# Feed-forward with tokens stationary: gate and up columns side by side as one 512-column moving operand, the result transposed, and conversions ahead moved behind the activation

## The chip, the cores and the metric

The kernel runs on one core of one Trainium2 chip. The metric is the device time of one execution in microseconds (us). Three runs of the kernel before took 1474.69 to 1477.07 us, with a median of 1476.81.

## What is computed

The reference is a stack of three blocks on 256 tokens of width 1024, all in float32. The first two are "macaron" layers: a feed-forward, a mixer, a feed-forward, each between RMS norms, with a residual sum. The mixer of layer 0 joins stick-breaking attention and a causal convolution; that of layer 1 is gated linear attention. The third block has adaptive modulation from a condition vector, one mixer of sparse attention and retention, and one feed-forward. So there are five feed-forwards, and all have the same form:

```python
def swiglu(x, w_in, w_out):
    a, b = jnp.split(x @ w_in, 2, axis=-1)
    return (jax.nn.silu(a) * b) @ w_out
```

Here `x` is 256 x 1024, the hidden width is 2816 (11 x 256), `a` is called the gate and `b` the up projection. In the third block gate and up are two weights. Every weight is used once, so all weights pass from HBM through the core once.

## The kernel before

**Precision.** A float32 product is made of three TensorE products: each operand is split in `hi` (a copy rounded to the engine's faster 32-bit type) and `lo` (what is left). `mm3` (L268) makes hi x hi, hi x lo and lo x hi into one sum. Weights are split as they arrive: `feed_cv` (L230) lets ScalarE write `hi` (L246) and VectorE `lo` (L247). Activations are kept transposed, features on partitions, as `xh` and `xl`.

**The weight stream.** `weight_plan` (L101) lists all weights as chunks of at most 128 x 1024 elements in the order of their use. `feed_dma` (L221) issues a chunk's load on SP's queue into one of four raw buffers (`NRAW`). `feed_cv(n)` converts all chunks up to `n`, and a chunk's load is issued when the buffer four chunks back is split. `nxt` (L251) hands out the next chunks. With `ahead` on, it also lets conversions run on, by one more than it hands out, up to a lead of `pos["depth"]`, 14 chunks in a feed-forward (28 buffers `s4` for hi and lo). `catch_up(n)` (L265) queues up to `n` more conversions within the same lead. The order of the calls is the order of the work on each engine: the schedule is manual, and an engine does its instructions in the order in which the program wrote them.

**A feed-forward** (`ffn`, L666) goes through the 2816 hidden columns in 11 blocks `j` of 256. For block 0, tokens are stationary: 128 tokens by 128 features of `xh` or `xl` are the weights of the array, and 256 columns of the gate or up chunk move (L684 to L688). The result has tokens on partitions; its product `u` is transposed on TensorE (L721) and split into `hh` and `hl` (`split_sb`, L531). For blocks 1 to 10, the weight chunk is stationary, 128 features by 128 hidden columns, and 256 tokens move (`wproj2`, L536): 48 matmuls for the gate (`pa`) and 48 for up (`pb_`). The result has hidden columns on partitions, as the output projection needs it, so nothing is transposed. The norm's factor per token, `x.r`, is then needed along the columns: `nz.rows()` (L426) spreads it with four matmuls into `x.rb`, VectorE multiplies the gate by it (L729), ScalarE applies SiLU (L730), VectorE multiplies by up (L745). The last feed-forward has a norm that is already applied (`x.r` and `x.rb` are `None`), and skips the factor.

The output projection of block `j - 1` stands in block `j`, behind its matmuls (`fpart`, L706): 24 matmuls with `hh` or `hl` stationary and 512 output columns moving, into four PSUM banks `f`. The projections of the last three blocks (`NH`) come at the end as `pieces`, first those of token half 0, then those of half 1. `boundary` (L491) takes these pieces and puts the next stage's norm, transposes and first conversions among them. In `each`, three steps of a side job (the modulation vector, `ada_step`, L619) are queued at the start of a block.

**PSUM** has eight banks `pb` of 128 x 512. The small tiles of a feed-forward (`sg`, `u`, `hh`, `hl`, the side job's) share 16 buffers `s2`.

## Time and profile before

| | |
|---|---|
| Median of three runs | 1476.81 us |
| The profiled execution | 1476.34 us |
| Its span, first to last instruction | 1474.6 us |
| TensorE busy | 1440.0 us, 98% |
| VectorE busy | 1000.3 us, 68% |
| ScalarE busy | 764.5 us, 52% |
| GpSimd busy | 259.5 us, 18% |
| HBM read | 277.90 MB, 189 GB/s over the span |
| mean granted TensorE clock | 0.992 |

In the profile PE is TensorE, PEld its weight loads, ACT ScalarE, DVE VectorE, POOL GpSimd, and SP the engine whose queue issues the weight loads. L12 is line 12 of the program. Matmuls are pipelined, and a matmul's record is longer than the time until the next one can start; the pace is therefore read from one start to the next, or as the length of a stretch over the number of matmuls in it. The trace's times are counted from the first instruction.

### The profile page before, as it was taken

What the parts mean: (1) busy time and instruction counts of PE and PEld (TensorE: products, weight loads), DVE (VectorE), ACT (ScalarE), POOL (GpSimd) and SP (SyncE); (2) the same over time, 40 slices, a digit from 0 to 9 for tenths busy, and PEclk for the clock granted to TensorE, in tenths of its full rate; (3) what the DMA queues carried; (4) which work ended last, traced back from release to release, by engine and by line L of the source; (5) the groups of instructions that cost most, each with busy time, mean ns of one, the idle gap of its engine ahead of it and who ended that gap; (6) DMA issues with size and microseconds to landing.
All of it is one profiled execution on the core that took longest, in us unless ns stands there. A gap on an engine that the chain in (4) does not pass through costs nothing. (4 is left out here: it accounts for less than half of the span.)

```text
span 1474.6 us, 24444 instructions
## 1 busy us (share of the span) xinstructions
PE 1440.0 (98%) x9623; PEld 1314.8 (89%) x9623; DVE 1000.3 (68%) x1348; ACT 764.5 (52%) x1182; POOL 259.5 (18%) x339
## 2 busy tenths in 40 slices
PE   9999998699999999999999999999999999999997
PEld 8999988579999999999888899998988877899997
DVE  6777658977776667766577677765596865566542
ACT  6554356756543364443663655545643664565431
POOL 3010025812000031000234110001132230200001
PEclk9999999899999999999999999999999999999999
DMA  8887644227887568775542488763565554387540
GB/s 276 275 279 250 188 144 130 71 86 241 286 260 234 172 223 265 231 237 173 163 144 72 129 282 261 259 207 116 164 198 169 165 170 157 101 262 240 183 129 29
DMA packets 194948, 281.03 MB, mean 191 GB/s; under 512 B 12381, under 2 KB 148241, under 8 KB 194834
## 3 DMA queue, kind: packets, MB, share of 16 engines
q1 hardware_dynamic: 184386, 248.87, 53.5%
q0 software_dynamic: 10048, 30.03, 6.2%
q8 instruction: 75, 1.23, 0.3%
q10 hardware_dynamic: 400, 0.57, 0.1%
q14 instruction: 39, 0.32, 0.1%
HBM read 277.90 MB, written 1.05 MB: 189 GB/s over the span
## 5 line engine op out<-in xcount | busy, mean ns | idle before, releaser
L247 DVE TENSOR_TENSOR lo<-raw,hi 128x1024 fp32r<-128x1024 f32 (+1 forms) x461 | 549.5, 1219 | 237.2 <-ACT hi L246 204.0
L246 ACT ACTIVATE hi<-raw 128x1024 fp32r<-128x1024 f32 (+1 forms) x472 | 477.4, 1037 | 206.4 <-PE pb L271 69.2
L269 PE MATMUL pb<-xh,hi 128*128 128x256 f32 x1968 | 558.4, 284 | 0.1
L271 PE MATMUL pb<-xh,lo 128*128 128x256 f32 x1968 | 556.8, 283 | 0.0
L270 PE MATMUL pb<-xl,hi 128*128 128x256 f32 x1968 | 556.8, 283 | 0.0
L269 PEld LDWEIGHTS pb<-xh,hi 128*128 128x128 f32 x1968 | 376.3, 191 | 3.4 <-issue 1.3
L270 PEld LDWEIGHTS pb<-xl,hi 128*128 128x128 f32 x1968 | 376.4, 191 | 2.0
L271 PEld LDWEIGHTS pb<-xh,lo 128*128 128x128 f32 x1968 | 376.3, 191 | 0.2
L269 PE MATMUL pb<-hi,hh 128*128 128x512 f32 x440 | 172.1, 391 | 0.0
L270 PE MATMUL pb<-lo,hh 128*128 128x512 f32 x440 | 171.7, 390 | 0.0
L271 PE MATMUL pb<-hi,hl 128*128 128x512 f32 x440 | 171.2, 389 | 0.0
L626 POOL DMA_DIRECT2D ada<-in_w_ada_dram x96 | 51.8, 542 | 452.0 <-PE pb L271 278.8
L532 ACT ACTIVATE hh<-u 128x512 fp32r<-128x512 f32 x50 | 31.6, 632 | 134.4 <-DVE u L745 132.5
L271 PEld LDWEIGHTS pb<-hi,hl 128*128 128x128 f32 x440 | 82.6, 188 | 17.5
L269 PEld LDWEIGHTS pb<-hi,hh 128*128 128x128 f32 x440 | 82.8, 188 | 15.9
L270 PEld LDWEIGHTS pb<-lo,hh 128*128 128x128 f32 x440 | 82.8, 188 | 15.3
L269 PE MATMUL pb<-hi,xh 128*128 128x512 f32 x224 | 91.5, 408 | 0.0
L271 PE MATMUL pb<-hi,xl 128*128 128x512 f32 x224 | 88.1, 393 | 0.0
L270 PE MATMUL pb<-lo,xh 128*128 128x512 f32 x224 | 88.0, 393 | 0.0
L730 ACT ACTIVATE sg<-sg 128x512 f32<-128x512 f32 x40 | 25.3, 632 | 109.8 <-DVE sg L729 109.8
L631 DVE SCALAR_TENSOR_TENSOR adacc<-ada,sc,adacc 128x512 f32<-128x512 f32 x84 | 63.0, 750 | 2.0
L331 POOL TENSOR_TENSOR rs_y<-rs_v,mhalf 128x1 f32<-128x1 f32 x30 | 16.9, 564 | 259.0 <-DVE rs_v L330 258.0
(314 smaller groups left out, 1726.2 us busy)
## 6 DMA issues: line engine op xcount, KB each, us to landing
raw<-in_ffn_w_in_dram SPq DMA_DIRECT2D x176, 512.0 KB, 5.0
raw<-in_ffn_w_out_dram SPq DMA_DIRECT2D x88, 512.0 KB, 4.7
raw<-in_w_in_dram SPq DMA_DIRECT2D x56, 512.0 KB, 4.2
ada<-in_w_ada_dram POOLq DMA_DIRECT2D x96, 256.0 KB, 4.5
raw<-in_gla_w_in_dram SPq DMA_DIRECT2D x24, 512.0 KB, 4.2
raw<-in_w_ffn_gate_dram SPq DMA_DIRECT2D x22, 512.0 KB, 4.8
raw<-in_w_ffn_up_dram SPq DMA_DIRECT2D x22, 512.0 KB, 5.0
raw<-in_w_ffn_down_dram SPq DMA_DIRECT2D x22, 512.0 KB, 4.0
```

Of the source, the lines that this page charges most:

```text
L246: act.activation(hv, r, AF.Copy)
L247: lo_on.tensor_tensor(lv, r, hv, op=ALU.subtract)
L269: pe.matmul(o, lh, rh, start=start, stop=False)
L270: pe.matmul(o, lh, rl, start=False, stop=False)
L271: pe.matmul(o, ll, rh, start=False, stop=stop)
L331: pool.tensor_tensor(y, v, mhalf[:, :1], op=ALU.pow)
L532: act.activation(hi, full, AF.Copy)
L626: pool.dma_start(t, w_ada[kt * 128:(kt + 1) * 128, cb * 512:(cb + 1) * 512])
L631: dve.scalar_tensor_tensor(ada["acc"], in0=t, scalar=sc[:, kt:kt + 1], in1=ada["acc"], op0=ALU.mult, op1=ALU.add)
L730: act.activation(sg, sg, AF.Silu)
```

## The change

Four things change together.

- The plan of a feed-forward: in place of chunks `fa` (gate) and `fb` (up) of 4 x 128 features by 256 columns, there are four chunks `fi` a block, each 2 x 128 features by 512 columns, 256 gate columns beside the 256 up columns of the same block. Each is loaded by two DMAs of 256 KB.
- All blocks are computed as block 0 was, with tokens stationary, and gate and up move together: one matmul has 512 columns and fills one bank. Per block and token half the bank holds gate | up.
- `gated(j, p)` applies SiLU with the norm's factor per partition and makes the product; `turn(j)` transposes it into one bank and splits it. `turn(j - 1)` stands behind the first chunk of block `j` (`TJ = 0`). For block 10 it is done in two halves among the pieces. `nz.rows()` is no longer called here.
- Conversions ahead: the calls of the first and the last chunk of a block (`ahead=i not in (TJ, 3)`) queue none beyond their own chunk; instead `catch_up(2)` stands behind `turn` and behind `gated`.

In the prologue of the kernel, block 0's first chunks are converted in slices of 512 columns accordingly.

```diff
 PRF = (0, 0, 2)
 CT, CS = (2, 2), (0, 1)
 CU = (0, 1, 2)
+TJ = 0
 DEPTH = (14, (10, 9), (10, 10), (10, 10))
 NT = 2
 LO, CL = ((1, 0), (1, 1)), 1
@@ -120,13 +121,11 @@
 
     def ffn(wa, wb, b0, wo):
         for j in range(NJ + 1):
-            if j == 0:
-                for k0 in (0, 4):
-                    cols("fa", wa, 0, 256, k0, 4)
-                    cols("fb", wb, b0, 256, k0, 4)
-            elif j < NJ:
-                tall("fa", wa, j * 256)
-                tall("fb", wb, b0 + j * 256)
+            for k0 in range(0, 8 if j < NJ else 0, 2):
+                rs = slice(k0 * 128, (k0 + 2) * 128)
+                src = [w[rs, c0:c0 + 256].rearrange("(k p) c -> p k c", p=128) for w, c0 in ((wa, j * 256),
+                                                                                             (wb, b0 + j * 256))]
+                plan.append(("fi", src, 2, 512))
             for i in range(2 if 0 < j <= NJ - NH else 2 * NH if j == NJ else 0):
                 cols("fo", wo, 0, 1024, 2 * (min(j - 1, NJ - NH)) + i, 1)
 
@@ -223,7 +222,12 @@
             i = pos["dma"]
             _, src, nk, n_ = plan[i]
             r = raws.tile([128, WCH], F32, tag="raw", name="raw")
-            nc.sync.dma_start(r[:, :nk * n_].rearrange("p (k c) -> p k c", k=nk), src)
+            rv = r[:, :nk * n_].rearrange("p (k c) -> p k c", k=nk)
+            if isinstance(src, list):
+                for g in range(2):
+                    nc.sync.dma_start(rv[:, :, g * 256:(g + 1) * 256], src[g])
+            else:
+                nc.sync.dma_start(rv, src)
             raw_t[i] = r
             pos["dma"] += 1
 
@@ -667,41 +671,53 @@
         x = nz.x
         hp = {}
 
-        def split_h(u):
-            hh, hl = s2([128, 2, S], F32R, name="hh"), s2([128, 2, S], F32R, name="hl")
-            split_sb(hh, hl, u)
-            return hh, hl
-
-        chs = nxt("fa", "fb", "fa", "fb", ahead=False)
-        pt, u0 = [], []
+        chs = nxt("fi", "fi", "fi", "fi", ahead=False)
+        p0 = []
         for t in range(2):
-            p = pp()
+            p = pb()
             ks = KO if t and not nz.early else range(8)
             for n_, kk in enumerate([*ks, None]):
-                for g in range(2):
-                    if kk is not None:
-                        hi, lo = chs[2 * (kk // 4) + g]
-                        pe.matmul(p[g][:, :S], x.h[:, kk, tsl(t)], hi[:, kk % 4], start=n_ == 0, stop=False)
-                        pe.matmul(p[g][:, :S], x.h[:, kk, tsl(t)], lo[:, kk % 4], start=False, stop=False)
-                    if n_:
-                        k0 = ks[n_ - 1]
-                        pe.matmul(p[g][:, :S], x.l[:, k0, tsl(t)], chs[2 * (k0 // 4) + g][0][:, k0 % 4], start=False,
-                                  stop=kk is None)
+                if kk is not None:
+                    hi, lo = chs[kk // 2]
+                    pe.matmul(p, x.h[:, kk, tsl(t)], hi[:, kk % 2], start=n_ == 0, stop=False)
+                    pe.matmul(p, x.h[:, kk, tsl(t)], lo[:, kk % 2], start=False, stop=False)
+                if n_:
+                    k0 = ks[n_ - 1]
+                    pe.matmul(p, x.l[:, k0, tsl(t)], chs[k0 // 2][0][:, k0 % 2], start=False, stop=kk is None)
                 if t == 0 and n_ in TB:
                     nz.trans(1, [TB.index(n_)])
-            pt.append(p)
+            p0.append(p)
             if t == 0:
                 nz.spread(1)
                 nz.evac(1)
                 nz.scale(1)
                 catch_up(CU[2])
-        for t in range(2):
-            sg = s2([128, S], name="sg")
-            act.activation(sg, pt[t][0][:, :S], AF.Silu, scale=1.0 if x.r is None else x.r[t])
-            u = s2([128, S], name="u")
-            dve.tensor_tensor(u, sg, pt[t][1][:, :S], op=ALU.mult)
-            u0.append(u)
         f = None
+        us = {}
+
+        def gated(j, p):
+
+            sg, u = s2([128, 2, S], name="sg"), s2([128, 2, S], name="u")
+            for t in range(2):
+                act.activation(sg[:, t], p[t][:, :S], AF.Silu, scale=1.0 if x.r is None else x.r[t])
+                dve.tensor_tensor(u[:, t], sg[:, t], p[t][:, S:], op=ALU.mult)
+            us[j] = u
+
+        def turn(j, ts=(0, 1)):
+
+            u = us[j]
+            if 0 in ts:
+                hp[j] = s2([128, 2, S], F32R, name="hh"), s2([128, 2, S], F32R, name="hl")
+            hh, hl = hp[j]
+            pr = pb()
+            pv = two(pr)
+            for t in ts:
+                for i in range(2):
+                    pe.transpose(pv[:, i, tsl(t)], u[:, t, i * 128:(i + 1) * 128], ident)
+            sl = slice(ts[0] * 128, (ts[-1] + 1) * 128)
+            split_sb(hh[:, :, sl], hl[:, :, sl], pv[:, :, sl])
+            if 1 in ts:
+                us.pop(j)
 
         def fpart(j, i, ch, t, n):
             hh, hl = hp[j]
@@ -709,29 +725,23 @@
             mm3(f[t][n], hh[:, i, tsl(t)], hl[:, i, tsl(t)], ch[0][:, 0, cs], ch[1][:, 0, cs],
                 j == 0 and i == 0, j == NJ - 1 and i == 1)
 
+        gated(0, p0)
+        p0 = None
         for j in range(1, NJ):
             if each and j > 1:
                 each()
-            pa = wp("fa", x)
-            if j == 1:
-                nz.rows()
-                pr = pb()
-                for i in range(2):
-                    for t in range(2):
-                        pe.transpose(pr[:, i * S + t * 128:i * S + (t + 1) * 128], u0[t][:, i * 128:(i + 1) * 128],
-                                     ident)
-                hp[0] = split_h(two(pr))
-            chb = nxt("fb", "fb")
-            sg = s2([128, 2, S], name="sg")
-            if x.rb is None:
-                act.activation(sg, two(pa), AF.Silu)
-            else:
-                dve.tensor_tensor(sg, two(pa), bc2(x.rb), op=ALU.mult)
-                act.activation(sg, sg, AF.Silu)
-            pb_ = pb()
-            wproj2(pb_, chb, x)
+            pj = pp()
+            for i in range(4):
+                ch = nxt("fi", ahead=i not in (TJ, 3))
+                for t in range(2):
+                    smm(pj[t], t, ch, 2 * i, 8, x.h, x.l)
+                if i == TJ:
+                    turn(j - 1)
+                    catch_up(2)
             if f is None:
                 f = [pp(), pp()]
+            gated(j, pj)
+            catch_up(2)
             if j < NJ - NH + 1:
                 for i in range(2):
                     ch = nxt("fo")
@@ -741,16 +751,17 @@
                 hp.pop(j - 1)
             if each:
                 ada_sum()
-            u = s2([128, 2, S], name="u")
-            dve.tensor_tensor(u, sg, two(pb_), op=ALU.mult)
-            hp[j] = split_h(u)
         cho = nxt(*["fo"] * (2 * NH))
 
         def pieces(t):
             def part(j, n):
                 for i in range(2):
                     fpart(j, i, cho[2 * (j - NJ + NH) + i], t, n)
-            return [(lambda j=j, n=n: part(j, n)) for n in range(2) for j in range(NJ - NH, NJ)]
+            todo = [(lambda j=j, n=n: part(j, n)) for n in range(2) for j in range(NJ - NH, NJ)]
+            if t == 0:
+                todo[1:1] = [lambda: turn(NJ - 1, (0,))]
+                todo[3:3] = [lambda: turn(NJ - 1, (1,))]
+            return todo
         return f, pieces
 
 
@@ -1526,14 +1537,15 @@
     nz.trans(0)
     feed_dma(4)
     for i in range(4):
-        cv_t[i] = tuple(s4([128, WCH], F32R, name=n_).rearrange("p (k c) -> p k c", k=4) for n_ in ("hi", "lo"))
+        cv_t[i] = tuple(s4([128, WCH], F32R, name=n_).rearrange("p (k c) -> p k c", k=2) for n_ in ("hi", "lo"))
     for k in range(8):
         nz.evac1(0, k)
-        for i in (k // 4 * 2, k // 4 * 2 + 1):
-            hi, lo = (z[:, k % 4] for z in cv_t[i])
-            rv = raw_t[i][:, k % 4 * 256:(k % 4 + 1) * 256]
-            act.activation(hi, rv, AF.Copy)
-            (pool if i % 2 and k in KS else dve).tensor_tensor(lo, rv, hi, op=ALU.subtract)
+        hi, lo = (z[:, k % 2] for z in cv_t[k // 2])
+        rv = raw_t[k // 2][:, k % 2 * 512:(k % 2 + 1) * 512]
+        act.activation(hi, rv, AF.Copy)
+        for g in range(2):
+            c = slice(g * 256, (g + 1) * 256)
+            (pool if g and k in KS else dve).tensor_tensor(lo[:, c], rv[:, c], hi[:, c], op=ALU.subtract)
     for i in range(4):
         raw_t.pop(i)
     pos["cv"] = 4
```

## Rows read from the trace of the kernel before

**Rows 1.** The page: busy us (share) of TensorE; granted clock in 40 slices.
```profile
PE 1440.0 (98%) x9623; PEld 1314.8 (89%) x9623; DVE 1000.3 (68%) x1348; ACT 764.5 (52%) x1182; POOL 259.5 (18%) x339
...
PEclk9999999899999999999999999999999999999999
```

**Rows 2.** Stretches of TensorE: start:end, length, busy (instructions touched), clock, DMA, GB/s.
```profile
395.41:406.92 11.51, 11.51 (x97) 1.00 0.88 284
...
200.38:204.47 4.09, 4.09 (x20) 1.00 0.71 231
...
805.97:811.55 5.58, 5.58 (x27) 1.00 0.07 23
```

**Rows 3.** Stretches from block 1, four feed-forwards: PE, PEld, DVE, ACT, POOL, clock, DMA.
```profile
22.80:58.80 36.00, 36.00 (x260) 34.03 (x259) 24.96 (x26) 21.40 (x25) 6.11 (x12) 1.00 0.88 289
343.50:379.50 36.00, 36.00 (x259) 34.08 (x258) 26.01 (x28) 20.35 (x24) 3.22 (x6) 1.00 0.91 301
848.34:884.34 36.00, 36.00 (x260) 34.08 (x259) 26.50 (x30) 19.23 (x22) 3.62 (x7) 1.00 0.89 286
1291.17:1327.17 36.00, 36.00 (x260) 34.08 (x259) 24.63 (x24) 22.14 (x26) 0.00 (x0) 1.00 0.84 269
```

**Rows 4.** Timeline of TensorE at transposes: start, us, operation, tiles, count.
```profile
538.82 0.78 PE L432 MATMUL pb<-dg,ones 128*128 128x128 f32 x4
539.43 0.60 PE L721 MATMUL pb<-ident,u 128*128 128x128 f32 x4
...
805.62 0.60 PE L525 MATMUL pb<-ident,oy 128*128 128x128 f32 x4
805.97 0.48 PE L269 MATMUL pb<-hi,xh 128*128 128x512 f32 x1
...
1296.93 0.60 PE L721 MATMUL pb<-ident,u 128*128 128x128 f32 x4
1297.28 0.36 PE L269 MATMUL pb<-xh,hi 128*128 128x256 f32 x1
```

**Rows 5.** Lines L700 and L702: count, duration in ns (min/median/max), first and last start.
```profile
L700 ACT ACTIVATE sg<-pb,rs_y x8: 457/469/477, 22.0 to 848.5; 128x256 f32<-128x256 f32 x8
...
L702 DVE TENSOR_TENSOR u<-sg,pb x10: 410/414/421, 23.5 to 1292.2; 128x256 f32<-128x256 f32 x10
```

**Rows 6.** Timeline of ScalarE: start, us, operation, count, idle before and its releaser.
```profile
7.99 0.42 ACT L1535 ACTIVATE hi<-raw 128x256 fp32r<-128x256 f32 x1 [1.08 <-DMA raw<-in_ffn_w_in_dram]
...
373.94 1.06 ACT L246 ACTIVATE hi<-raw 128x1024 fp32r<-128x1024 f32 x1 [2.80 <-DMA raw<-in_ffn_w_out_dram]
...
378.39 0.63 ACT L730 ACTIVATE sg<-sg 128x512 f32<-128x512 f32 x1 [1.89 <-DVE sg L729]
...
504.87 1.99 ACT L246 ACTIVATE hi<-raw 128x1024 fp32r<-128x1024 f32 x2
```

**Rows 7.** Timeline of VectorE: splits of weights, merged runs of up to four.
```profile
49.78 1.23 DVE L247 TENSOR_TENSOR lo<-raw,hi 128x1024 fp32r<-128x1024 f32 x1 [0.24 <-ACT hi L246]
...
371.17 1.22 DVE L247 TENSOR_TENSOR lo<-raw,hi 128x1024 fp32r<-128x1024 f32 x1 [0.26 <-ACT hi L246]
...
505.95 2.36 DVE L247 TENSOR_TENSOR lo<-raw,hi 128x1024 fp32r<-128x1024 f32 x2 [0.26 <-ACT hi L246]
...
873.47 4.62 DVE L247 TENSOR_TENSOR lo<-raw,hi 128x1024 fp32r<-128x1024 f32 x4
...
1313.51 4.63 DVE L247 TENSOR_TENSOR lo<-raw,hi 128x1024 fp32r<-128x1024 f32 x4 [0.26 <-ACT hi L246]
```

**Rows 8.** The raw buffers, 344 to 380 us: issue ns (min/median/max); landing.
```profile
L226 SPq DMA_DIRECT2D raw<-in_ffn_w_in_dram x12: 367/373/379, 344.3 to 376.3; - x12
...
DMA to landing us min/median/max: 3.5/5.3/6.8
```

**Rows 9.** Timeline of TensorE in the mixer of layer 0.
```profile
291.68 0.79 PE L271 MATMUL pb<-hi,ml 128*128 128x512 f32 x1 [2.52 <-DVE ml L898]
```

**Rows 10.** The stretch behind that wait, columns as in rows 3.
```profile
292.27:295.68 3.41, 3.41 (x9) 2.63 (x8) 3.41 (x6) 3.36 (x6) 3.10 (x5) 0.50 0.00 0
```

## Prediction

> **What bounds the kernel now.** I read the page's busy times first: TensorE is busy for 1440.0 of 1474.6 us, and the granted clock stands at 9 in nearly every slice [rows 1]. So a change counts where it alters the time of TensorE's own stream, or stops that stream. Next I read that stream by stretches [rows 2]. A feed-forward's block of 256 hidden columns is 96 matmuls of 256 columns in 11.51 us: 120 ns from one to the next. Matmuls of 512 columns with tokens stationary, which another stage runs already, take 4.09 us for 18: 227 ns each. No pause is left inside such a block, so the change cannot remove one; it can only make the stream shorter and put pauses into it. Last I read the other engines where a feed-forward begins: there, DMA is busy 84 to 91% of the time [rows 3], so weights come about as fast as they can be loaded, and ScalarE waits for them (2.80 us in one place [rows 6]).
>
> **What the stream loses and gains.** Each of the five feed-forwards has 11 blocks. A block's 96 matmuls become 48 (8 contraction steps, 2 token halves, 3 products) of 512 columns: 48 x 0.227 = 10.90 us for 11.51, so 0.61 us less, and 55 x 0.61 = 33.6 us less in all [rows 2].
>
> The result now has tokens on partitions, so it must be transposed. Before, only block 0 did this, in 5 groups of four transposes. Now there are 50 such groups, and 10 of two for the last blocks. Four transposes take 0.35 us until the next matmul starts, between wide matmuls as between narrow ones [rows 4]. Behind them the wide matmuls need a moment to regain their pace: 24 of them take 5.58 us and not 24 x 0.227 = 5.45 [rows 2], so a group costs 0.48 us. With narrow neighbours I estimate 0.43 (some 0.08 us late behind it), and 0.61 is what four other matmuls of 128 columns took, the row scale's, with a wait in them [rows 4]; these are my two ends. A group of two saves two steps of 0.11 us: 0.27 us. Sum: 50 x 0.48 + 10 x 0.27 - 5 x 0.43 = 24.5 us more (22 to 32).
>
> The call that spreads the row scale along columns goes in the four feed-forwards that have it: 0.61 us each [rows 4], 0.43 where nothing waits; I take 4 x 0.5 = 2.0 us less. TensorE's stream is thus 33.6 + 2.0 - 24.5 = **11.1 us shorter** (4 to 14).
>
> A word on the Trainium skill: its page "TensorE: Matmul & The Clock Gate", section "Back-to-back issue gap", gives an isolated matmul's gap as N / 2.4 plus 2.5 ns, by which doubling the width would save 2.5 ns for each pair, 2640 x 2.5 ns = 6.6 us in place of 33.6, and the change would lose some 16 us by its transposes. The rows disagree: 2 x 120 - 227 leaves 13 ns for a pair, with both widths read at the full clock.
>
> **ScalarE, VectorE and the queues.** ScalarE's SiLU becomes two of 128x256 for one of 128x512: 0.47 us each [rows 5] for 0.63 [rows 6], 0.3 us more in a block. VectorE loses the multiplication by the row scale and makes the product in two pieces of 0.41 us [rows 5]. Neither engine is the bound over a block; only the moment counts at which each reaches this work. Both work in program order, and between these operations stand the weight conversions (hi on ScalarE, 1.06 us [rows 6]; lo on VectorE, 1.23 us [rows 7]), each of which can wait for its DMA, or for a buffer that TensorE frees.
>
> The price is set by a new wait. In the kernel before, block j's product was needed, split, when its output projection began: one block later. Now TensorE itself transposes it after the first chunk of the next block, that is 24 x 0.227 + 12 x 0.227 = 8.2 us after the block's end (2.7 us after block 0 and after block 9, behind which no output projection stands). Queued behind a late transpose is all of TensorE's stream.
>
> I number a feed-forward's chunks from 0; block 0 takes 0 to 3, a later block four and then two for an output projection. By the calls, chunks up to 6 are converted ahead when block 1 begins (up to 5 in the first feed-forward). In block 1 six more are queued ahead of its SiLU (two by catch_up, two by each of the two calls with ahead on), and six behind it; in block 2 six ahead again. So block 2's SiLU stands behind chunk 24 (23 in the first). Until the lead reaches the limit of 14 chunks, these wait for DMA, not for buffers.
>
> When does chunk 24 land? Four raw buffers go round, so its load starts when chunk 20 has been split: at 372.39 us in the second feed-forward, 878.09 in the fourth and 1318.14 in the fifth, and 51.01 for chunk 19 in the first (start and duration of [rows 7]). From issue to landing it takes 5.3 us (3.5 to 6.8) [rows 8]. From there hi takes 1.06, lo 1.25 behind it, and the two products 0.8 (the SiLUs, 0.94, run beside lo): 3.1 us. Ready at 59.4, 380.8, 886.5 and 1326.5. Block 2's transposes are due 36.4 us after block 1 begins (2 x 10.9 + 2 x 5.45 + 2.7 + 2 x 0.48), and block 1 begins 0.6 us earlier than before, at the start of each window of [rows 3] less 0.6: due at 58.6, 379.3, 884.1 and 1327.0. TensorE would wait 0.8, 1.5, 2.4 and 0 us. But the first conversions of block 1 now stand behind block 0's transposes, some 2.8 us later than before; followed from chunk to chunk, in steps of 5.3 us of load and 2.3 of conversion, about 1.0 us of that is left at chunk 20. I take 1.8 + 2.5 + 3.4 + 0.5 = **8.2 us of waiting** (0.6, if loads come at 3.5 us and nothing is late; 21, at 6.8 us and the whole 2.8 late). The third feed-forward follows another one and begins with four more chunks converted, so nothing is late there. From block 3 on the limit of 14 chunks lets only as much be queued as TensorE has freed, and the wait is over.
>
> The second new wait is at the end. After block 10 its second SiLU runs, then catch_up queues two conversions, and only then comes the split of the transposed half. From the end of block 10: SiLU until 0.8 us, two hi until 2.7 (1.99 for two [rows 6]) and two lo, from 1.8 on, until 4.2 (2.36 for two [rows 7]); then half of hl, 0.4: 4.6 us. TensorE is there after two pieces of 6 x 0.227 and two transpose groups, at 3.3 us, and asks for hl with its third matmul, at 3.8. That is 0.8 us, in four feed-forwards (the last has no weights left to convert): **3.2 us** (0 to 6). Before, the split stood ahead of these two conversions, so that cover goes.
>
> Two DMAs for one chunk: an issue holds SP's queue for 0.37 us [rows 8], and beside the loads SP issues only a few constants; the packets keep their 1 KB rows. The second half starts 0.4 us later, which is inside the bounds above. In the prologue, block 0's first conversions need one buffer instead of two (ScalarE waited 1.08 us for the second [rows 6]), but a piece is twice as wide: I take 0, from -1 to +1 us. PSUM: a block's two banks and one for transposes fit into the four that the outputs leave, each freed before it is asked for, so 0; if not, it is the price of the transposes' own wait.
>
> **Sum.** -11.1 + 8.2 + 3.2 = +0.3 us. The profiled execution took 1476.34 us (span 1474.6), 0.5 us under the median of 1476.81. 1476.3 + 0.3 = 1476.6: **about 1477 us, no change that can be told**; 0.2% (2.95 us) is about what a measurement of this kernel can tell from none, so "same" runs from 1473.9 to 1479.8. The forecast's own range is 1471 to 1484.
>
> **Rivals.**
> *The product is always in time.* Loads come faster than 5.3 us, as the row-scale steps no longer stop the conversions. For it: before, ScalarE sat idle for 1.89 us at 378.39 until the scaled SiLU could run [rows 6], a stop that goes. Against it: DMA is 84 to 91% busy. Then -11.1 and the ends' 0 to 3.2: **1467 us** (1465 to 1469).
> *The product is late and the clock falls* (the other side). One mechanism: block 2's SiLU behind chunk 24. It decides from a total wait of 11.3 us there on (1479.8 - 1476.3 + 11.1 - 3.2). With 6.3 us from issue to landing, between the median and the worst, and 1.5 us of lateness, the waits are 3.3 + 4.0 + 4.9 + 2.0 = 14.2 us. In another stage TensorE waited 2.52 us [rows 9], and behind that its granted clock was 0.50 (the 1.2 GHz level), nine matmuls in 3.41 us [rows 10] for 2.0; at two places that is 2.8 us. -11.1 + 14.2 + 3.2 + 2.8 = 9.1: **1485 us**.
> *The width saves less here.* At the 5.58 us for 24 of [rows 2], which stand behind transposes, a block takes 11.16 us, and 55 blocks save 19 us in place of 33.6: **1491 us**. Against it: the pace settles within a few matmuls.
> *The change does not do what it says.* Half as many matmuls and four transposes a block follow from the loops, so that is excluded; that the conversions stand behind the activation's work holds for the two calls named, not for the six conversions ahead of it, which the forecast prices.
>
> **Chances.** Forecast 0.51 (0.06 of it faster than 1473.9, 0.32 same, 0.13 slower); in time 0.26, all faster; late with the clock 0.21 and less saved 0.02, all slower. Faster 0.06 + 0.26 = 0.32; same 0.32; slower 0.13 + 0.21 + 0.02 = 0.36. The range takes in most of both sides: 1465 to 1489.
>
> **What would show it.** 48 matmuls of 512 columns in about 10.9 us a block; four transposes in 0.35 us; no row-scale matmuls in the feed-forwards; a TensorE wait of 1 to 4 us ahead of block 2's transposes, released by VectorE's u, in the first, second and fourth feed-forward and none in the third; about 0.8 us before the last block's first piece, released by hl. I am wrong if the blocks take 11.2 us or more, if those waits are missing, or if one stands in every block.

## The result, and the profile after

The changed kernel takes 1487.9 us (median of 4 runs, 1484.2 to 1490.3) for 1476.8 before: a ratio of 1.0073, 95% interval 1.0054 to 1.0091. It is slower by 11.1 us, where the forecast said no change that can be told (1477 us, its own range 1471 to 1484; the wide range, 1465 to 1489, holds it). The time lies where the rival put it that has the product late and the clock low behind it (1485 us); two things that also stopped TensorE, a PSUM bank ahead of block 3 and the late split of block 1, were not in that rival. The profiled execution took 1487.56 us, span 1485.8.

The page of the changed kernel: TensorE's busy time, and its granted clock in 40 slices.
```profile
PE 1432.4 (96%) x7167; PEld 1192.4 (80%) x7167; DVE 978.5 (66%) x1359; ACT 765.2 (51%) x1221; POOL 258.4 (17%) x339
...
PEclk9999999999999999999999999999999999999999
```
Against [rows 1]: TensorE has 7.6 us less to do in a span that is 11.2 us longer. So the stream did become shorter, and some 19 us of standing still came in. The row of the clock hides what follows, since a slice is 37 us long.

Where it stands still shows when each feed-forward is one stretch, from its first transposes of the residual to those ahead of the next stage. Columns: start:end, length, TensorE's busy time, clock, DMA share, GB/s. The kernel before:
```profile
5.32:196.76 191.44, 190.08 (x1335) 0.99 0.77 249
327.49:516.97 189.48, 189.48 (x1345) 1.00 0.72 232
516.97:706.62 189.65, 189.65 (x1346) 1.00 0.70 221
832.34:1022.04 189.70, 189.70 (x1348) 1.00 0.69 219
1271.58:1466.99 195.41, 194.53 (x1373) 1.00 0.51 159
```
The changed kernel, the same five:
```profile
5.26:205.65 200.39, 189.79 (x843) 0.98 0.75 237
336.39:529.76 193.37, 189.15 (x853) 0.99 0.71 227
529.76:717.32 187.56, 186.97 (x854) 1.00 0.71 224
841.37:1034.65 193.28, 189.55 (x855) 0.99 0.67 214
1284.65:1477.94 193.29, 192.41 (x885) 1.00 0.51 161
```
The third and the fifth are 2.1 us shorter each. The first, second and fourth, which follow the start or a mixer, are 9.0, 3.9 and 3.6 us longer: length less busy time is 10.6, 4.2 and 3.7 us there, and was 1.4, 0 and 0. The mixers between them are not touched; the one of layer 1 is 1.7 us shorter here, and was as short in a run of the kernel before (e4).

A block that nothing disturbs, as stretches of TensorE in the third feed-forward (columns as in [rows 3]): 12 matmuls, then 36 behind the four transposes, then the whole block with its output projection.
```profile
561.98:564.70 2.72, 2.72 (x13) 2.20 (x12) 2.15 (x3) 1.39 (x2) 0.00 (x0) 1.00 0.90 299
565.05:573.35 8.30, 8.30 (x40) 6.85 (x38) 7.48 (x9) 5.20 (x6) 1.07 (x2) 1.00 0.93 289
561.98:578.79 16.81, 16.81 (x78) 13.90 (x76) 13.43 (x15) 10.14 (x12) 1.61 (x3) 1.00 0.94 306
```
2.72 + 0.35 + 8.30 = 11.37 us for 48 wide matmuls and four transposes, where 96 narrow ones took 11.51 [rows 2]. These terms of the sum hold, and so does the group's 0.35 of [rows 4].

TensorE's own rows where a feed-forward stumbles, in the changed kernel (start, us, operation, tiles, count, idle before and its releaser): the first (50 to 70 us), the second (381 and 392) and the fourth (887 to 898), and the end of the first (194 to 195).
```profile
50.66 0.50 PE L273 MATMUL pb<-hi,hh 128*128 128x512 f32 x1 [0.49 <-ACT hh L536]
...
57.17 0.34 PE L306 MATMUL pb<-ident,rows 124*128 124x124 f32 x2
62.95 0.80 PE L273 MATMUL pb<-hi,xh 128*128 128x512 f32 x1 [5.44 <-DVE u L703]
63.55 0.63 PE L274 MATMUL pb<-lo,xh 128*128 128x512 f32 x1
...
69.83 0.66 PE L716 MATMUL pb<-ident,u 128*128 128x128 f32 x4 [1.39 <-DVE cols L307]
...
194.09 0.40 PE L274 MATMUL pb<-lo,hh 128*128 128x512 f32 x1
195.07 0.50 PE L275 MATMUL pb<-hi,hl 128*128 128x512 f32 x1 [0.58 <-DVE hl L537]
...
380.96 0.50 PE L275 MATMUL pb<-hi,hl 128*128 128x512 f32 x1 [0.37 <-DVE hl L537]
...
392.24 0.77 PE L716 MATMUL pb<-ident,u 128*128 128x128 f32 x4 [3.27 <-DVE u L703]
...
887.34 0.50 PE L275 MATMUL pb<-hi,hl 128*128 128x512 f32 x1 [1.78 <-DVE hl L537]
...
898.27 0.77 PE L716 MATMUL pb<-ident,u 128*128 128x128 f32 x4 [1.30 <-DVE u L703]
```
The row at 57.17 is the two column loads: `col_load` transposes 124 and 84 rows of small parameters, each into a PSUM bank of its own, from which VectorE copies them; the first feed-forward does this ahead of block 3.

Read the operand, not only the releaser. At 62.95 the matmul reads weights and x alone, and yet waits for u: it writes a PSUM bank, which is free when u has been computed from it. At 392.24 and 898.27 the transposes read u itself. At 380.96 and 887.34 an output projection wants hl. From start to start, less the usual step, a stop costs 0.16 us more than the idle time in brackets, which is counted from a modelled end (0.40 more at 69.83, behind the half clock; 5.44 as it stands at 62.95). So they cost 0.65 + 0.81 (hl, two rows on, at 52.04) + 5.44 + 1.79, then 0.53 + 3.43, then 1.94 + 1.46: 8.7, 4.0 and 3.4 us in the three feed-forwards, **16.1 us**. At the ends of four feed-forwards a piece waits 0.74 to 0.82 us for hl, 3.1 us in all.

The clock behind these waits (stretches of TensorE: length, busy, clock, DMA share, GB/s):
```profile
62.95:67.81 4.86, 4.86 (x11) 0.50 0.91 315
392.76:396.50 3.74, 3.74 (x12) 0.58 0.77 215
888.45:891.44 2.99, 2.99 (x9) 0.50 0.82 267
```
A clock of 0.50 is the 1.2 GHz level, as in [rows 10]: 427 ns a matmul for 227. With the slow first steps behind a stop it costs 2.4, 1.6 and 1.8 us: **5.8 us**.

Why u is late: ScalarE's rows ahead of block 2's SiLU, in the first and in the fourth feed-forward.
```profile
57.29 1.06 ACT L250 ACTIVATE hi<-raw 128x1024 fp32r<-128x1024 f32 x1 [2.81 <-DMA raw<-in_ffn_w_out_dram]
58.79 1.06 ACT L250 ACTIVATE hi<-raw 128x1024 fp32r<-128x1024 f32 x1 [0.45 <-DMA raw<-in_ffn_w_in_dram]
60.26 1.06 ACT L250 ACTIVATE hi<-raw 128x1024 fp32r<-128x1024 f32 x1 [0.41 <-DMA raw<-in_ffn_w_in_dram]
61.22 0.82 ACT L702 ACTIVATE sg<-pb,rs_y 128x256 f32<-128x256 f32 x2
...
892.93 1.06 ACT L250 ACTIVATE hi<-raw 128x1024 fp32r<-128x1024 f32 x1 [3.84 <-DMA raw<-in_ffn_w_in_dram]
895.57 1.06 ACT L250 ACTIVATE hi<-raw 128x1024 fp32r<-128x1024 f32 x1 [1.57 <-DMA raw<-in_ffn_w_in_dram]
896.53 0.82 ACT L702 ACTIVATE sg<-pb,rs_y 128x256 f32<-128x256 f32 x2
```
In the first, block 2's last input matmul had started at 49.78 us. Its SiLU ran at 61.22, behind chunks 21 to 23, each of which waited for its DMA. TensorE read none of them before 81 us. Such waits stood there before, too (2.80 us in [rows 6]); then no product was wanted right behind them.

In the fourth, the wait of 3.84 us goes back to VectorE. Its rows, and that of SP's queue:
```profile
883.30 1.53 DVE L635 SCALAR_TENSOR_TENSOR adacc<-ada,sc,adacc 128x512 f32<-128x512 f32 x2
...
886.61 0.68 DVE L537 TENSOR_TENSOR hl<-pb,hh 128x512 fp32r<-128x512 f32 x1
887.21 4.62 DVE L251 TENSOR_TENSOR lo<-raw,hi 128x1024 fp32r<-128x1024 f32 x4
...
888.45 0.88 SPq L228 DMA_DIRECT2D raw<-in_ffn_w_in_dram  x2
```
The four lo are those of chunks 19 to 22. Chunk 19's hi was done at 883.6, but its lo stood behind the adaptation's steps (the side job `ada_step`) and block 1's hl, until 888.4. Only then was its raw buffer free for chunk 23, which was issued at 888.45 and converted from 892.93 on. The load itself was not slow: there the median from issue to landing was 4.4 us.

### The profile page after: what moved, and what is told of

Read it like the earlier page. It is cut to its first block, busy times and chain, and to the rows that moved or that the text cites. A ratio compares the mean times of both kernels' runs of the same rounds, so it can differ in the third digit from the quotient of the medians.

```text
span 1485.8 us, 19900 instructions
## 1 busy us (share of the span) xinstructions
PE 1432.4 (96%) x7167; PEld 1192.4 (80%) x7167; DVE 978.5 (66%) x1359; ACT 765.2 (51%) x1221; POOL 258.4 (17%) x339
## 4 chain that ended last, share of the span: by engine, by line
PE 78%; DVE 9%; DMA 5%; issue 3%; ACT 3%; SPq 1%; POOL 0%; DVEq 0%; POOLq 0%; ACTq 0%
PE pb L273 23%; PE pb L275 23%; PE pb L274 23%; DMA raw<-in_ffn_w_in_dram 4%; DVE lo L251 3%; ACT hi L250 2%; DVE y L804 2%; PE pb L716 1%; DVE yb L804 1%; PE pb L683 1%; PE pb L682 1%; PE pb L686 1%; PE pb L396 1%; DMA raw<-in_w_in_dram 1%; DMA raw<-in_ffn_w_out_dram 1%
## 5 line engine op out<-in xcount | busy, mean ns | idle before, releaser
L273 PE MATMUL pb<-hi,xh 128*128 128x512 f32 x1024 | 409.0, 399 | 5.5 <-DVE u L703 5.4
L275 PE MATMUL pb<-hi,xl 128*128 128x512 f32 x1024 | 401.3, 392 | 0.0
L274 PE MATMUL pb<-lo,xh 128*128 128x512 f32 x1024 | 400.4, 391 | 0.0
L273 PEld LDWEIGHTS pb<-hi,xh 128*128 128x128 f32 x1024 | 193.3, 189 | 46.2 <-DVE u L703 5.6
L275 PEld LDWEIGHTS pb<-hi,xl 128*128 128x128 f32 x1024 | 193.1, 189 | 42.1 <-DVE xl L485 0.2
L274 PEld LDWEIGHTS pb<-lo,xh 128*128 128x128 f32 x1024 | 193.6, 189 | 38.3 <-DVE lo L251 0.3
L703 DVE TENSOR_TENSOR u<-sg,pb 128x256 f32<-128x256 f32 x110 | 44.9, 420 | 120.9 <-ACT sg L702 120.6
L702 ACT ACTIVATE sg<-pb,rs_y 128x256 f32<-128x256 f32 x88 | 40.7, 472 | 135.4 <-PE pb L275 134.7
L273 PE MATMUL pb<-xh,hi 128*128 128x256 f32 (+2 forms) x368 | 105.1, 286 | 0.0
L274 PE MATMUL pb<-xl,hi 128*128 128x256 f32 (+2 forms) x368 | 104.0, 283 | 0.0
L275 PE MATMUL pb<-xh,lo 128*128 128x256 f32 (+2 forms) x368 | 104.0, 283 | 0.0
```

The lines of the kernel that those rows point to most:

```text
L273: pe.matmul(o, lh, rh, start=start, stop=False)
L274: pe.matmul(o, lh, rl, start=False, stop=False)
L275: pe.matmul(o, ll, rh, start=False, stop=stop)
L702: act.activation(sg[:, t], p[t][:, :S], AF.Silu, scale=1.0 if x.r is None else x.r[t])
L703: dve.tensor_tensor(u[:, t], sg[:, t], p[t][:, S:], op=ALU.mult)
```

## The experiments

All times are medians: the changed kernel 1487.9 us; the kernel before, measured again beside the experiments, 1476.9 to 1478.4. Intervals are those of the ratio to that median.

**e1, fewer conversions ahead.**
```diff
                 if i == TJ:
                     turn(j - 1)
-                    catch_up(2)
+                    if j > 2:
+                        catch_up(2)
```


> The changed kernel without the two conversions that are queued behind the transposes of blocks 0 and 1; all else as it is. Block 2's SiLU then stands behind chunk 19 in place of 23 in the first feed-forward (20 for 24 in the others), block 1's split behind 15 for 17. Theory (SiLU and split are late because they are queued behind conversions that wait for DMA, and the clock falls behind the waits): in blocks 2 and 3 of the first, second and fourth feed-forward the changed kernel lost 11.4 + 5.9 + 5.3 = 22.6 us against its own later blocks; all of it goes: 1465 us (1463 to 1470). Rival (two DMAs for a chunk make the loads slow, whatever the order): the pauses stay, now for the weights themselves, 1485 us or more. Rival (TensorE's stream is no shorter, the transposes cost what the width gives): the pauses go, and the time stops at that of the kernel before, 1476 or above.


Measured: 1479.8 us (1474.7 to 1482.4 in 10 runs), ratio 1.0009 (0.9993 to 1.0024). 8.1 us go, not 22.6. The second feed-forward has no wait left in blocks 1 and 2, nor has the fourth. In the first, TensorE's row shows another one:
```profile
65.92 1.11 PE L716 MATMUL pb<-ident,u 128*128 128x128 f32 x4 [7.07 <-DVE cols L307]
```
VectorE in the same kernel, where the product is long done:
```profile
53.47 0.74 DVE L703 TENSOR_TENSOR u<-sg,pb 128x256 f32<-128x256 f32 x2
...
64.44 1.22 DVE L251 TENSOR_TENSOR lo<-raw,hi 128x1024 fp32r<-128x1024 f32 x1 [1.87 <-ACT hi L250]
65.58 0.43 DVE L307 COPY cols<-pb 128x124 f32<-128x124 f32 x2
```
u was ready at 54.2. The transposes waited for a bank that the column loads hold until VectorE copies them, and those copies stand behind five conversions that wait for DMA. In block 3 of the second and fourth feed-forward, hl is now late (2.2 and 2.6 us): on VectorE it stands behind a conversion and the three steps of the adaptation's sum (L635, 2.32 us). So the late product is one cause; two more stood behind it, the column loads' banks and the adaptation's steps.

**e2, the order undone.** `ahead=True` at all four chunks, and both new `catch_up(2)` taken out.


> The second part of the change undone: the conversions ahead are queued at every chunk of the new width, with no catch_up behind the transposes or behind the product. Block 2's SiLU then stands two chunks further back (behind 25 in the first feed-forward, 26 in the others), block 1's split behind 19 or 20. Theory: a chunk costs some 1.5 to 2 us there, so 3 to 4 us more wait before block 3's transposes (or its first matmul) and 2 to 3 us more before block 1's output projection in three feed-forwards, and 0.8 us less at the end of four: 1498 us (1493 to 1506). Rival (the order costs nothing, the loads set the pace): 1484 to 1488 us.


Measured: 1484.6 us (1482.8 to 1485.9), ratio 1.0044 (1.0028 to 1.0059): the theory's 1498 fell. Its waits were added up where they replace each other. In the first feed-forward block 1's split came 2.7 us late for the output projection, and in the second 1.1, but such a stop lets the product of block 2 catch up: the transposes of the second then wait 1.3 us for 3.4, and in the fourth one stop of 3.5 us for hl stands for the two of 1.94 and 1.46. And the ends no longer wait, which is about what the time gained (3.3 us). So putting those four conversions behind the activation's work gained nothing here, and two more ahead of block 2's SiLU cost nothing; four fewer (e1) were worth 8.1 us.

**e3, the column loads behind the transposes of block 2.**
```diff
                     turn(j - 1)
+                    if late:
+                        late.pop()()
                     catch_up(2)
```


> The changed kernel with the two column loads of the first feed-forward (two transposes of 124 and 84 rows, their two PSUM banks, and what follows them) moved from ahead of block 3 to behind its transpose group. Theory (there the 5.4 us wait is one for a PSUM bank: the column loads took the two free ones, so block 3's first matmul needs the bank that block 2's product frees): block 3 starts at 57.2 us, its transposes wait some 3.4 us for the same late product, and about 4 us of the first feed-forward's loss go: 1483 us (1481 to 1485). Rival (banks play no part): the same wait before block 3's first matmul, 1487 us. Rival (the column loads are the whole loss there): 1477 us.


Measured: 1488.1 us (1483.7 to 1490.3), ratio 1.0064 (1.0042 to 1.0087). TensorE's rows there:
```profile
62.27 0.77 PE L718 MATMUL pb<-ident,u 128*128 128x128 f32 x4 [2.64 <-DVE u L705]
62.88 0.27 PE L306 MATMUL pb<-ident,rows 124*128 124x124 f32 x1
69.70 0.40 PE L306 MATMUL pb<-ident,rows 84*128 84x84 f32 x1 [6.55 <-DVE hl L537]
```
The first half came as expected: block 3 starts at 56.75 without a wait, and the transposes wait 2.64 us for u. But the second column load then needs a bank itself, the one that the transposes' split still holds, and stops the stream for 6.55 us. The time says "banks play no part", the rows say the opposite: the shortage only moved.

**e4, the kernel before with two DMAs for each input chunk** (each of half the rows).


> The kernel before with each feed-forward's input chunk loaded by two DMAs of half its size in place of one, the packets unchanged. Theory (the number of issues costs nothing that TensorE sees): 1476 to 1478 us, no wait in blocks 1 to 3. Rival (two issues for a chunk slow the loads, and that made the changed kernel's pauses): 1480 us or more, with TensorE waiting in blocks 2 and 3.


Measured: 1476.2 us, ratio 0.9991 (0.9982 to 1.0001). "No wait in blocks 1 to 3" missed: in block 3 of the first feed-forward, right behind the column loads, TensorE waited 0.52 us for sg and later 1.06 for u, which the profile of before does not show, and 0.43 in block 1 of the second. In the time the number of issues costs nothing that can be told; as the cause of the 11 us, that rival is out.

**e5, e1 with the column loads at block 5**, where the first feed-forward's conversions no longer wait for DMA. The adaptation's steps begin there too, so the two move together.
```diff
-        if len(started) == 2:
+        if len(started) < 4:
+            return
+        if len(started) == 4:
             col_load(1, 124)
```


> The kernel with fewer conversions ahead, and the two column loads and all steps of the adaptation's sum begun two blocks later, at block 5 of the first feed-forward, where no conversion waits for DMA any more. With the column loads ahead of block 3 that kernel still lost there 7.35 us in the first chunk, 0.4 in the transposes and 1.0 at the half clock behind them, 8.8 us. Theory (the column loads' transposes hold two PSUM banks until VectorE, queued behind conversions, copies them; TensorE waits for such a bank): all of it goes, 1471 us (1469 to 1473). Rival (the product of block 2 is what is late there): the wait stays with the product's name, 1477 to 1480 us.


Measured: 1469.1 us (1467.3 to 1471.9), ratio 0.9942 (0.9924 to 0.9961). As the theory has it, and faster than before the change: the first feed-forward takes 189.98 us for e1's 197.84.

**e6, e5 with two conversions moved behind the last split.**
```diff
             gated(j, pj)
-            catch_up(2)
+            if j < NJ - 1:
+                catch_up(2)
...
-                todo[3:3] = [lambda: turn(NJ - 1, (1,))]
+                todo[3:3] = [lambda: turn(NJ - 1, (1,)), lambda: catch_up(2)]
```


> The kernel of the run before, and the two conversions that stand between the last block's product and its split queued behind the split. Theory: the wait for hl at the end, 0.75 us in each of four feed-forwards, goes: 3.0 us less than the run before, 1468 us. Rival (what is saved there is waited for at the boundary behind it): the same time as the run before.


Measured: 1504.6 us, ratio 1.0182 (1.0164 to 1.0199). The edit did not do what its text says. The call for the last six chunks still converted two ahead of the split, so the 0.75 us stayed; and by then the limit let two more in. ScalarE's row of this kernel shows the first of these, ahead of the boundary's squares:
```profile
194.39 1.06 ACT L250 ACTIVATE hi<-raw 128x1024 fp32r<-128x1024 f32 x1 [9.86 <-PE pb L275]
195.36 0.67 ACT L346 ACTIVATE sq<-pb,rs_y 128x512 f32<-128x512 f32 x1
```
and TensorE's what that costs:
```profile
199.26 1.09 PE L396 MATMUL pb<-ident,h 128*128 128x128 f32 x4 [4.28 <-DVE h L367]
```
The conversion waited 9.86 us for a buffer that TensorE frees with its last output projections, and the norm of the finished half stood behind it. At four boundaries this wait comes to some 17 us, of 37.9 by which the profiled span is over e5's; the clock behind the first is 0.76 for 6.7 us, and the rest was not taken apart. The same fault as in the change, with a buffer in place of a DMA.

**e7, e6 with the adaptation's steps and the column loads behind the split of each block.**


> The kernel of the run before, and the three steps of the adaptation's sum (2.3 us on VectorE) queued behind the split of the transposes in each block in place of ahead of it. Theory (in block 3 of the second and fourth feed-forward hl stood behind these steps, and TensorE waited 2.2 and 2.6 us for it): 4 to 5 us less than the run before, 1464 us (1462 to 1466), no wait of TensorE over 0.5 us left in any feed-forward's blocks 1 to 10, and each of the first four is at 187 to 189 us. Rival (hh stands behind a conversion that waits for DMA in the same place): 0 to 1 us less.


Measured: 1503.1 us, 1.5 less than e6. The second feed-forward gains 3.3 us (its hl no longer waits, 2.2 us in e6), the first loses 1.6, since the column loads ask for banks there at the wrong moment again, as in e3. The absolute numbers fell with e6.

**e8, e7 with each input matmul of blocks 1 to 10 as two of 256 columns.**


> The kernel of the run before, each input matmul of 512 columns in blocks 1 to 10 done as two of 256 (gate columns, then up columns), everything else as it is. This prices the width alone. Theory (120 ns for 256 columns, 227 for 512): 0.61 us more in each of 50 blocks, 30.5 us: 30 us over the run before, 1494 us. Rival (a matmul of 512 columns between transposes takes the 232 ns that 24 of them show): 0.37 us a block, 18 us more, 1482 us. The Trainium skill (TensorE: Matmul & The Clock Gate, section Back-to-back issue gap) would give, with 2.5 ns for a matmul, 50 x 48 x 2.5 ns = 6 us more, 1470 us.


Measured: 1532.8 us, 29.65 us over e7: 0.593 us a block where 0.61 was expected. The third feed-forward alone is 5.99 us longer than e7's, 0.60 a block. This is the width alone, 12.4 ns for each pair of narrow matmuls. The Trainium skill's 2.5 ns a matmul (TensorE: Matmul & The Clock Gate, section Back-to-back issue gap), which the page gives for an isolated matmul, would have made it 6 us; here the measurement decides against it.

**e9, e5 with the end done anew.**
```diff
-        cho = nxt(*["fo"] * (2 * NH))
+        cho = nxt(*["fo"] * (2 * NH), ahead=False)
...
+                todo[3:3] = [lambda: turn(NJ - 1, (1,)), lambda: feed_cv(pos["use"] - 7 + pos["depth"])]
```


> The kernel with fewer conversions ahead and the column loads at block 5, and the end of a feed-forward done anew: the call for the last six chunks converts nothing ahead, and what it converted ahead (up to the same chunk, no further) is queued behind the split of the last block's transposes. The earlier attempt left this call as it was, which converted ahead of the split all the same, and let two more chunks in ahead of the boundary's work. Theory: no 4.4 us wait for h at the boundary, no 0.75 us wait for hl before the last block's first piece in the four feed-forwards: 3.0 us less, 1466 us (1465 to 1467.5). Rival (what is saved is waited for at the boundary): 1469 us as without this edit. Rival (any conversion behind that split stands ahead of the boundary's work and costs there): 1480 us or more.


Measured: 1464.4 us (1464.2 to 1465.2), ratio 0.9921 (0.9906 to 0.9936). The profiled spans differ from e5's by 3.1 us (1465.6, 1462.5), as expected; the medians by 4.8. No piece at an end waits for hl.

**e10, e9 with the sum's steps behind the split**, the column loads still ahead of block 5.


> The kernel of the run before, and the three steps of the adaptation's sum behind the split in each block; the column loads stay ahead of block 5. Theory: the wait for hl in block 3 of the second feed-forward (1.27 us in the profile of the kernel without these two edits, 2.2 in others) goes, no wait over 0.5 us is left in any feed-forward: 1 to 2 us less, 1465 us (1463.5 to 1466). Rival (the steps then hold up the conversions' lo on VectorE, and weights come late): the same or more than the run before, with TensorE waiting for lo.


Measured: **1462.1 us** (1461.4 to 1464.8), ratio 0.9908 (0.9891 to 0.9925), the best version. Its five feed-forwards, columns as in the stretches above:
```profile
5.20:193.44 188.24, 186.73 (x843) 0.99 0.76 245
324.21:511.12 186.91, 186.91 (x853) 1.00 0.73 235
511.12:697.78 186.66, 186.66 (x853) 1.00 0.70 225
821.80:1009.10 187.30, 187.30 (x856) 1.00 0.72 230
1258.65:1451.85 193.20, 192.32 (x885) 1.00 0.50 161
```
TensorE stands still only where it did before, at the start of the first and at the last one's edges.

**e11, e10 without the transposes of the product.**


> The kernel of the run before without TensorE's transposes of the product: the split reads u as it lies, so the output projections work with an operand that is not transposed. This prices the transposes alone, with no wait left beside them. Theory (0.35 us for four, and 0.12 us more for the 36 matmuls behind them): 50 x 0.47 + 10 x 0.23 = 26 us less than the run before, 1439 us (1437 to 1442). Rival (the slower 36 matmuls are slow for another reason): 50 x 0.35 + 10 x 0.18 = 19 us less, 1446 us.


This kernel no longer computes the function; it serves for a price alone. Measured: 1439.4 us, 22.7 less than e10. That lies between the two expectations where some of the saving is given back: the second feed-forward now waits some 3.1 us for hh and hl, and the last mixer ran 2.3 us longer. The third, undisturbed, takes 181.37 us for 186.66: 5.3 us, and 5 x 5.3 = 26.5. One block there (TensorE, columns as above), its input matmuls and the whole:
```profile
535.48:546.36 10.88, 10.88 (x50) 1.00 0.91 305
535.48:551.80 16.32, 16.32 (x74) 1.00 0.84 273
```
48 wide matmuls with nothing between them take 10.88 us, and a block 16.32 for the changed kernel's 16.81: four transposes cost 0.49 us, all told.

**e12, the column loads (and the adaptation's steps) at block 5 alone**, conversions as in the change.


> The changed kernel with its conversions ahead as they are, and the column loads and the adaptation's sum begun at block 5 only. Theory (two causes that stand one behind the other: the late product, and the banks): block 3 of the first feed-forward starts without a wait, its transposes wait some 3.4 us for u as those of the second and fourth feed-forward, and the half clock stays behind them; some 4 us of the changed kernel's 1487.9 go: 1484 us (1481 to 1486). Rival (the column loads are the whole of it there): 1478 us. Rival (the late product is the whole of it): 1488 us.


Measured: 1478.4 us (1474.3 to 1484.1 in 10 runs), ratio 1.0009 (0.9991 to 1.0028). The size is that of the rival, the rows are those of the theory: block 3 starts without a wait, and the product is still late.
```profile
62.13 1.08 PE L716 MATMUL pb<-ident,u 128*128 128x128 f32 x4 [2.77 <-DVE u L703]
```
The first feed-forward stands still for 3.6 us in place of 8.7 (0.64 for block 1's hl, 2.93 here) and takes 194.55 us, 5.8 less. The other 3.2 us of the profiled spans' 9.0 lie mostly in the second and fourth, where only the phase of the adaptation's steps differs; why is not settled.

Together: fewer ahead alone takes 8.1 us off, columns late alone 9.5, both 18.8. The two add up within the spread of the runs (e1's ten lie between 1474.7 and 1482.4), so both were causes. "Columns late" holds the adaptation's steps too: that the banks and not the steps stopped the first feed-forward is read from the rows at 62.95 in the changed kernel and 65.92 in e1, not from a run that moves the loads alone.

## What of the prediction held, and what failed

The wide range, 1465 to 1489 us, holds 1487.9 only because it takes in a rival at 1485. The forecast itself, no change at 1477 with its own range up to 1484, did not come: the stream became shorter by at least what was reckoned, but the stops were more than twice as long.

- *The width and the transposes* held. 0.61 us a block: 0.593 (e8). 0.48 us a group: 0.49 (e11). Each of the five feed-forwards, free of waits, is shorter: their busy time falls from 953.4 to 939.9 us in e10, 13.5 us for the 11.1 forecast and inside its 4 to 14.
- *The end's wait*: 0.8 us forecast, 0.74 to 0.82 measured, in four feed-forwards.
- *The third and fifth feed-forward*: no wait forecast in the one and 0.5 us in the other; none in either.
- *PSUM, "each freed before it is asked for, so 0"*: this step failed. It counted a block's two banks and one for the transposes, and not the two that the first feed-forward's column loads take ahead of block 3. The four outputs, block 2's pair and the column loads are eight banks, so none is free, and the stream waits ahead of the block for a product that was to be needed only behind its first chunk: 5.44 us there, 1.79 for the column loads' copies, and half a clock behind. So the first chunk (2.7 us) no longer ran while the product was awaited, and with the copies that makes 4.5 us where the sum had 0. The rows at 62.95, 69.83 and 65.92 (e1) show it; in e3 the shortage moved, in e5 and e12 it is gone.
- *The waits at block 2's transposes*, 8.2 us: the mechanism was right, the size was short. Counted against TensorE's stream without the stops ahead of it, the product came 4.3, 4.0 and 5.2 us late in the first, second and fourth feed-forward, for 1.8, 2.5 and 3.4 forecast (due at 58.6, 388.3 and 893.1 us, there at 62.9, 392.2 and 898.3). The sum took from the kernel before, plus 1.0 us, the moment at which a raw buffer comes free. In the fourth, chunk 20's came free at some 889.6 us, for 888.1 by that rule (the feed-forward begins 9.0 us later than before); the adaptation's steps and block 1's split held up the conversions on VectorE.
- *Block 1's split* was not in the sum. Queued behind chunk 17 or 18, and in the second and fourth behind the adaptation's steps, it stopped the output projection for 0.53 to 1.94 us a place. e1 takes this from blocks 1 and 2, and in e10 no block has it. Such a stop comes off the later wait and does not add to it; that the fourth's stops total the 3.4 us of the forecast is luck.
- *The clock* was in a rival (2.8 us at two places) and not in the forecast: 5.8 us at three places.
- In sum, of the profiled execution's +11.2 us the five feed-forwards have +12.2 and the rest -1.0 (of it the mixer of layer 1 -1.7, which the change does not touch). The stops are 16.1 + 5.8 + 3.1 = 25.0, so some -12.8 of stream, against +8.2 + 3.2 - 11.1. The rival had 14.2 of waits and 2.8 of clock, and was nearest. (The wait from which it decides is 11.4 us by its own terms, not 11.3; nothing hangs on it.)

What stays open: why e12 also gained in the second and fourth feed-forward, what all of e6's loss consists of, how much of the columns' share in e5 and e12 is the adaptation's steps, and whether more raw buffers would have kept the product in time; that was not tried.

## What to carry to other kernels

When an engine that is nearly always busy is made to consume a product one step sooner, look up what stands ahead of that product on every in-order queue it passes, and what each of those waits for: a prefetch that waits for DMA, or for a buffer, holds up the work behind it, although nobody needs the prefetch yet. Count PSUM banks with every guest in the loop, side jobs too, and read a wait's operands to tell a bank from data. Waits on one chain replace each other and do not add up, but causes that stand one behind the other do: take them away one at a time and look at what is late next.

## What was not expected of the hardware

- A stop of 1.78 us was followed by half the clock, but only after four matmuls at the full pace or near it: from 887.34 us on, the steps are 0.34, 0.23, 0.23 and 0.31 us, then 0.43, and the matmuls from 888.45 to 891.44 us show 0.50. Behind 5.44 us (62.95) it stood at once, behind 3.27 us (392.24) after the transposes and two matmuls; behind 1.30 us (898.27) the steps stay at 0.23 to 0.24 after the first.
